# The up projections of a hybrid encoder layer: plain three-pass products in place of the seven-product scheme, and the gated first branch kept on chip

## The chip, the cores and the metric

The kernel runs on one core of a Trainium2 chip. The metric is the device time of one execution in microseconds (us). TensorE is called PE in the profile (PEld is its weight load), VectorE DVE, ScalarE ACT, GpSimd POOL and SyncE SP.

## The reference

One layer of a streaming encoder, for 528 prompt tokens (16 meta rows and 512 frames) and 64 sample tokens that share the weights; D_MODEL is 2048. All data is float32. Cut to what matters here:

```python
h = rms_norm(x, pre_gain)
(g_q, g_k, g_v, g_z, g_r, s_q, s_k, s_v, s_z, m_gla, m_sb) = jnp.split(h @ w_in, IN_SPLITS, axis=-1)
...
y_gla = (o_gla * jax.nn.silu(g_z)) @ w_up_gla
...
y_sb = (o_sb.reshape(B, T, SB_W) * jax.nn.silu(s_z)) @ w_up_sb
merged = jax.nn.sigmoid(m_gla) * y_gla + jax.nn.sigmoid(m_sb) * y_sb
y = x + rms_norm(merged @ w_o, post_gain)
```

`w_up_gla` and `w_up_sb` are 1024 x 2048 each, `w_o` is 2048 x 2048. The meta rows are dropped behind the up projections, so that these work on 576 token columns.

## The kernel before

Activations lie transposed: features on the 128 partitions, tokens in the free dimension. A float32 product is made of three passes of rounded parts: an operand is split into a high part (a cast to fp32r, "hi") and a remainder (the operand minus its high part, "lo"), and a product is hi·hi + hi·lo + lo·hi, three matmuls of 128x288 (`passes`).

The products run as *pairs* of two 128-column tiles of the output. Each pair's weights come from HBM into a `raw` tile (1 MB, three buffers) by two loads on SP. A pair is a list of *units*: a unit takes four k-tiles of weights, a 128x512 block, which ScalarE casts to `whi` and of which VectorE takes the remainder `wlo` (a ring of four each), and TensorE then multiplies. The streams `convert`, `remain`, `combine` and `multiply` issue these steps for all units of the program in order.

Pairs are computed by a Strassen-like scheme (`strassen`), with two halves of the tokens, the two column tiles and the two halves of k as the 2x2 blocks: seven products in place of eight. Its price is sums: of weight blocks (`raw<-raw` on VectorE), of products (`out`, `u` from the PSUM banks `b`), and of the activations, which are made once per operand as seven blocks (H11, H21, H22 and T1 to T4).

Stages, in order: the norm; the input projection (`w_in`), with the attention branches in the background; the up projections, first 8 pairs of `w_up_gla` (key "og"), then 8 pairs of `w_up_sb` (key "os"); and 8 pairs of `w_o`, whose results are transposed, scaled and added to x. An up pair has k = 8 tiles, so seven units of 12 matmuls. A w_o pair has 14 units.

What touches the change:

- `operands` loads the eight tiles of a branch from DRAM scratch into one `stage` tile, makes the sums (two on POOL, two on VectorE), and `split` turns each of seven blocks into hi and lo, in the places of old activation tiles (tags such as h0h; a block in the trace is `h0h`, `h6h` and so on). `RELEASE` says from which unit on such a place is free.
- `up_pair` with `done_gla` or `done_sb`: a finished column tile in `out` or `u` is multiplied by its gate (loaded from scratch as `gate`, with ScalarE's sigmoid). The first branch's result is stored to scratch (`d_yg`); in the second branch it is loaded again (`yg`), and POOL adds the two into a quarter of the merged tiles, `m_tile(0)` to `m_tile(3)` (`m<-out,yg`).
- `merged` takes those quarters as blocks of the w_o product: again sums and splits into hi and lo (`m<-m,m`); the items in `ON_POOL` are made by POOL, the others by VectorE. The order "first" of the first w_o pair begins with the blocks that are ready earliest.

What sets the order of the work is the planner (`Plan`): it keeps an estimated time for each engine and lets the stream with the earliest due time issue next (`UP_LEADS` and `WO_LEADS` shift the streams). The result is one fixed list per engine, in which an engine works strictly in order.

All instructions are recorded by one helper and have line 197 in the profile; they are told apart by their tiles.

Of the kernel before, what the change touches and what calls it, by code (L numbers as in the profile page):

```python
# [9 lines left out]
F32 = mybir.dt.float32  # L10
# [3 lines left out]
AF = mybir.ActivationFunctionType  # L14
# [3 lines left out]
P = 128  # L18
# [3 lines left out]
T = TP + DEC  # L22
# [3 lines left out]
KT = D // P  # L26
# [181 lines left out]
def hybrid_step_kernel(ctx: ExitStack, tc: tile.TileContext, a, o):  # L208
# [651 lines left out]
    opnd = {}  # L860
    halves = TO // 2

    def up_pair(src, p, key, done):
        outs, got = {}, {}
        depth = 2 if key == "og" else 3

        def put(ct, half, f, last):
            if ct not in outs:
                fourth = (2 * p + ct) % 4 == 3
                outs[ct] = pools["ev"].tile([P, T], F32, "u" if fourth else "out", bufs=1 if fourth else 3)[:, :TO]  # L870
            f(outs[ct][:, half * halves : half * halves + halves], slice(0, halves))
            if last:
                gated(ct, outs.pop(ct))

        def blocks(blk, k):
            return [x[:, k] for x in opnd[key, blk]]

        def gated(ct, t):
            done(2 * p + ct, t, got[ct], got[ct, "at"] + 0.1)

        def fetch(ct):
            got[ct] = pools[key].tile([P, TO], F32, "gate", bufs=depth)
            sync.dma_start(out=got[ct], in_=scratch["mg" if key == "og" else "ms", 2 * p + ct])
            t = got[ct, "at"] = plan.ready[got[ct].tensor.name]
            slower.append((t, "act", lambda x=got[ct]: act.activation(x, x, AF.Sigmoid), None))
            if key == "os":
                yg = pools[key].tile([P, TO], F32, "yg", bufs=depth)
                sync.dma_start(out=yg, in_=scratch["yg", 2 * p + ct])
                got[ct] = got[ct], yg

        def need(blk, q):
            first = KT if key == "os" else 0
            for b, x, c in ((H11, "stored", -4), (H21, "gated", -depth), (T1, "gated", 1 - depth), (T1, "stored", -3)):
                c += 2 * p + first
                if b == blk and c >= (first if x == "gated" else 0) and (x, c) not in made:
                    return False
            return (key, blk) in made

        strassen(src, 2 * p * P, 4, "up", blocks, halves, put, need, {"W12": lambda: fetch(0), "S1": lambda: fetch(1)})

    def done_gla(c, t, s, at):
        d = dram(("yg", c), TO)

        def f():
            dve.tensor_mul(t, t, s)
            sync.dma_start(out=d, in_=t)
            made.update(((x, c) for x in ("gated", "stored")))

        after("dve", f, slower, t=at)

    m_tiles = {}

    def m_tile(i, dtype=F32R):

        if i not in m_tiles:
            if i == 1:
                t = pools["os"].tile([P, 8 * halves], dtype, "m1")
# [5 lines left out]
    def done_sb(c, t, s, at):  # L923
        s, yg = s

        def f():
            dve.tensor_mul(t, t, s)
            after("pool", g, slower)

        def g():  # L930
            x, t2, yg2 = m_tile(c // 4, F32)[:, :, c % 4], *(z.rearrange("p (j t) -> p j t", j=2) for z in (t, yg))
            pool.tensor_add(x, t2, yg2)
            made.update((("gated", KT + c), ("stored", KT + c), ("m", c)))

        after("dve", f, slower, t=at)

    OG_TAGS = {H11: "h0h", H21: "h0l", T4: "h6h", T1: "h6l", T3: "h5h", H22: "h5l", T2: "h3h"}
    OS_TAGS = {H11: "h3l", H22: "h4h", T2: "h4l", T3: "h1h", T1: "h1l", H21: "h2h", T4: "h2l"}
    ON_POOL = (("T1", 0), ("T1", 1), (H22, 0), (T4, 0), (T3, 1))
    M_TAGS = {  # L940
        0: "h0h", 2: "h6h", 3: "h0l", (H11, 0): "h6l", (H11, 1): "h5h", (T1, 0): "h5l", (T1, 1): "h3h",
        (H21, 0): "h3l", (T4, 0): "h2l", (T3, 0): "h2h", (H22, 0): "h1l", (T2, 0): "h1h",
        (H21, 1): "h4h", (T4, 1): "h4l", (T3, 1): "h6h", (H22, 1): "h0h", (T2, 1): "h0l",
    }
    M_AFTER = {(T3, 1): ((T4, 0), (H22, 0)), (H22, 1): ((T3, 0), (T2, 0)), (T2, 1): ((T4, 1), (H22, 1))}
    RELEASE = {f"h{BLOCK_OF[x]}": n_in - 14 + 2 * i + 2 for i, x in enumerate(ORDERS["in"])}

    for p in range(8):
        up_pair(a["w_up_gla"][0], p, "og", done_gla)
    n_gla = len(units)  # L950
    for p in range(8):
        up_pair(a["w_up_sb"][0], p, "os", done_sb)
    n_up = len(units)

    RELEASE.update({OS_TAGS[BLOCK_OF[x]]: n_up - 7 + i + 1 for i, x in enumerate(ORDERS["up"])})
    wo = {}
    ends = {}

    def wo_pair(p):
# [20 lines left out]

        def free(name):
            if p == 0:
                return name == "W12" or ("m", 12 if name == "W11" else 13) in made
# [585 lines left out]
            yield from sb_chain(seq // 5, ORDER[seq % 5])  # L1569


    def split(key, blk, src, tags):
        tag = tags[blk]
# [3 lines left out]
        hi, lo = opnd[key, blk] = [t[:, x * 1152 : (x + 1) * 1152].rearrange("p (k t) -> p k t", k=4) for x in range(2)]  # L1577
        act.copy(hi, src)
        rests["dve"].append((plan.last, (key, blk), lo, src, hi))

    rests = {"dve": [], "pool": []}

    def second(eng):

        i = 0
        while True:
            yield lambda: len(rests[eng]) > i or len(done) == 4 * BLK
            if len(done) == 4 * BLK:
# [4 lines left out]
            (pool if eng == "pool" else dve).tensor_sub(lo, src, hi.bitcast(F32))  # L1593
            done.add(key)
            if key[0] != "os":
                made.add(key)

    done = set()

    def operands(key, tags):  # L1600

        x = pools["stage"].tile([P, 8, TO], F32, "stage")
        t3 = pools["stage"].tile([P, 4, halves], F32, "t3")
        for c in range(8):
            load(x[:, c], scratch[key, c])
        x11, x12, x21, x22 = (x[:, i : i + 4, j : j + halves] for i in (0, 4) for j in (0, halves))
        yield "pool"
        pool.tensor_sub(t3, x22, x12)
        yield "pool"
        pool.tensor_sub(x12, x12, x11)  # L1610
        yield from split(key, H11, x11, tags)
        yield from split(key, H21, x21, tags)
        yield (lambda: (key, H11) in done), "dve"
        dve.tensor_sub(x11, x22, x12)
        yield (lambda: (key, H21) in done), "dve"
        dve.tensor_sub(x21, x21, x11)
        for blk, src in ((T4, x21), (T1, x12), (T3, t3), (H22, x22), (T2, x11)):
            yield from split(key, blk, src, tags)
        yield lambda: (key, T2) in done

    def merged_split(blk, half, src):
        tag = M_TAGS[blk, half]
# [7 lines left out]
        rests["pool" if (blk, half) in ON_POOL else "dve"].append((plan.last, ("m", blk, half), lo, src, hi))  # L1630

    def merged():

# [42 lines left out]
    def background():  # L1676
# [29 lines left out]
        banks.quota = 1  # L1706
        plan.lead = UP_LEADS
        act.preload_act_table_set("sigmoid_and_others")
        pools["og"] = Region("og", "right")
        pools["stage"] = Region("stage", "right")  # L1710
# [4 lines left out]
        pools["stage"].close()  # L1715
        pools["os"] = Region("os", "right")
        made.update(("os", blk) for blk in range(BLK))
        for g, name in merged():
            plan.add(g, 0.0, name)

# [12 lines left out]
    def wo_open():  # L1733
        if "tl" in pools:
            return
        act.preload_act_table_set("natural_log_exp_and_others")
        for key in ("os", "og", "ev"):
# [152 lines left out]
```

## Time and profile before

| | before |
|---|---|
| runs | 1803.08, 1809.61, 1808.87 us, median 1808.87 |
| profiled execution | 1804.95 us, span 1803.1 us |
| busy share of the span | PE 92%, DVE 78%, ACT 50%, POOL 16% |
| mean granted TensorE clock | 0.968 |
| DMA | 233.57 MB, mean 130 GB/s |

The span runs from the first to the last instruction of the profiled execution; the profiled execution's own time has a little around it. Matmuls overlap one another (one is listed with some 0.3 us while the next starts 0.13 us later), so starts, and not durations, tell their rate. "idle <- X" in a row is the time that an engine waited, and what released it.

### The profile page before, as it was taken

To read this page: it belongs to the slowest core of one execution; us is meant where nothing else is said; L and a number is where in the kernel's file an instruction comes from. 1 tells how busy PE (TensorE), PEld (TensorE's weight loads), DVE (VectorE), ACT (ScalarE), POOL (GpSimd) and SP (SyncE) were. 2 spreads that over 40 slices of the span, in tenths; PEclk is the share of its full clock that TensorE was granted. 3 is DMA by queue.
4 is the path that set the end of the run, shared out by engine and by line. 5 is a ranking of instruction groups with operands and counts; after the bars stand their busy time and mean duration, and the time that the engine had idled before them with its cause. 6 is when DMAs were issued, how large, how long until landed. Compare 5 with 4: busy or idle time off the path is not lost.

```text
span 1803.1 us, 31606 instructions
## 1 busy us (share of the span) xinstructions
PE 1654.7 (92%) x11852; PEld 1592.3 (88%) x11852; DVE 1407.5 (78%) x2247; ACT 909.9 (50%) x1880; POOL 285.5 (16%) x342
## 2 busy tenths in 40 slices
PE   3799899899999999999999999999989987779995
PEld 1599899899999998999999999999989977679994
DVE  5877878786987887876666656676789999988777
ACT  4555444354444444456645554555455554445553
POOL 4600220120120120021111111111101013310002
PEclk9899899999999999999999999999999989889998
DMA  7054334334444334555454455444546654413326
GB/s 159 14 143 139 91 109 135 97 112 119 125 115 136 113 91 120 145 149 143 128 156 130 141 153 149 133 142 123 169 127 200 203 155 141 136 50 103 100 77 210
DMA packets 332068, 233.57 MB, mean 130 GB/s; under 512 B 21531, under 2 KB 297499, under 8 KB 330747
## 3 DMA queue, kind: packets, MB, share of 16 engines
q1 hardware_dynamic: 330884, 226.83, 43.8%
q10 hardware_dynamic: 1031, 4.72, 0.9%
q8 instruction: 93, 1.52, 0.4%
q14 instruction: 60, 0.49, 0.1%
HBM read 183.89 MB, written 47.62 MB: 128 GB/s over the span
## 4 chain that ended last, share of the span: by engine, by line
PE 80%; DVE 12%; issue 3%; DMA 2%; ACT 1%; POOL 1%; DVEq 0%; SPq 0%; ACTq 0%; POOLq 0%
PE b L197 80%; DVE wlo L197 4%; DVE raw L197 2%; DVE out L197 1%; DVE m L197 1%; DMA xt<-in_x_prompt 1%; DVE u L197 1%; DVE xr L197 1%; DVE x L197 0%; ACT whi L197 0%; POOL x L197 0%; DVE b L197 0%; DMA x<-d_gv 0%; DMA q<-d_gq 0%; DVE sv L197 0%
## 5 line engine op out<-in xcount | busy, mean ns | idle before, releaser
L197 ACT CAST whi<-raw 128x512 fp32r<-128x512 f32 x840 | 514.9, 620 | 593.8 <-PE b L197 430.2
L197 DVE TENSOR_TENSOR wlo<-raw,whi 128x512 fp32r<-128x512 f32 x840 | 603.2, 732 | 246.0 <-ACT whi L197 238.5
L197 DVE TENSOR_TENSOR raw<-raw 128x1024 f32<-128x1024 f32 (+2 forms) x305 | 326.9, 1074 | 8.2
L197 PE MATMUL b<-m,whi 128*128 128x288 f32 x896 | 185.1, 301 | 20.3 <-DVE m L197 8.5
L197 PEld LDWEIGHTS b<-m,whi 128*128 128x128 f32 x896 | 149.2, 195 | 21.3 <-DVE m L197 9.0
L197 PE MATMUL b<-h2h,whi 128*128 128x288 f32 (+1 forms) x416 | 128.4, 323 | 11.6 <-DVE u L197 10.7
L197 PE MATMUL b<-m,wlo 128*128 128x288 f32 x448 | 135.4, 302 | 0.8 <-DVE wlo L197 0.8
L197 PE MATMUL b<-h2l,whi 128*128 128x288 f32 (+1 forms) x416 | 122.3, 308 | 7.7 <-ACT h2l L197 6.9
L197 PE MATMUL b<-h6h,whi 128*128 128x288 f32 (+1 forms) x416 | 122.5, 308 | 6.3 <-ACT h6h L197 5.5
L197 PE MATMUL b<-h2h,wlo 128*128 128x288 f32 (+1 forms) x384 | 118.8, 309 | 6.0 <-DVE wlo L197 6.0
L197 PE MATMUL b<-h0h,whi 128*128 128x288 f32 (+1 forms) x416 | 120.9, 305 | 2.0 <-ACT whi L197 2.0
L197 PE MATMUL b<-h5h,whi 128*128 128x288 f32 (+1 forms) x416 | 122.4, 308 | 0.0
L197 PE MATMUL b<-h6l,whi 128*128 128x288 f32 (+1 forms) x416 | 118.4, 299 | 3.2 <-DVE h6l L197 3.2
L197 PE MATMUL b<-h3h,whi 128*128 128x288 f32 (+1 forms) x416 | 120.8, 304 | 0.0
L197 PE MATMUL b<-h6h,wlo 128*128 128x288 f32 (+1 forms) x384 | 115.4, 301 | 5.0 <-DVE wlo L197 5.0
L197 PE MATMUL b<-h4h,whi 128*128 128x288 f32 (+1 forms) x416 | 119.9, 302 | 0.0
L197 PE MATMUL b<-h0l,whi 128*128 128x288 f32 (+1 forms) x416 | 119.6, 302 | 0.0
L197 PE MATMUL b<-h1l,whi 128*128 128x288 f32 (+1 forms) x416 | 119.0, 300 | 0.0
L197 PE MATMUL b<-h1h,whi 128*128 128x288 f32 (+1 forms) x416 | 119.0, 300 | 0.0
L197 PE MATMUL b<-h5l,whi 128*128 128x288 f32 (+1 forms) x416 | 118.2, 298 | 0.0
L197 PE MATMUL b<-h3l,whi 128*128 128x288 f32 (+1 forms) x416 | 117.4, 296 | 0.0
L197 PE MATMUL b<-h4l,whi 128*128 128x288 f32 (+1 forms) x416 | 117.2, 296 | 0.0
(280 smaller groups left out, 4272.1 us busy)
## 6 DMA issues: line engine op xcount, KB each, us to landing
raw<-in_w_in SPq DMA_DIRECT2D x176, 512.0 KB, 5.0
raw<-in_w_o SPq DMA_DIRECT2D x32, 512.0 KB, 4.7
raw<-in_w_up_gla SPq DMA_DIRECT2D x16, 512.0 KB, 5.4
raw<-in_w_up_sb SPq DMA_DIRECT2D x16, 512.0 KB, 5.4
d_mg<-out SPq DMA_DIRECT2D x16, 288.0 KB, 2.1
d_ms<-out SPq DMA_DIRECT2D x16, 288.0 KB, 3.7
gate<-d_mg SPq DMA_DIRECT2D x16, 288.0 KB, 4.0
gate<-d_ms SPq DMA_DIRECT2D x16, 288.0 KB, 5.9
```

What stands on the lines that cost most here:

```text
L197: return real(*args, **kw)
```

## The change

Four things change in the code.

1. `plain` replaces `strassen` for the up projections: a pair is four units, each column tile's k-tiles 0 to 3 and 4 to 7. A unit multiplies its four k-tiles with both token halves, into two PSUM banks: 24 matmuls of 128x288. There are no sums of weights or products.
2. The operands are hi and lo of the tiles themselves: four blocks of two k-tiles for each branch, loaded through a `stage` tile with two buffers. No sums.
3. The gate multiplies straight from PSUM. In the first branch the product is written into the merged tiles, which now exist from the first branch on; in the second it is written over the gate, and one VectorE sum adds it to the merged tile. Store and load of `yg` are gone, and so is POOL's sum.
4. The sums and remainders of the merged blocks that POOL made are made by VectorE (`ON_POOL` is gone). The tags of the merged tiles are dealt anew.

The core of the diff:

```diff
+    GATES = 3
+    def plain(src, c0, blocks, done, need, start):
+        box = {}
+        add_load(box, "a", src, c0, 0)
+        def unit(c, q):
+            def mm(hi, lo):
+                if q == 0:
+                    start(c)
+                    for j in range(2):
+                        banks.take(box, (c, j))
+                for k in range(4):
+                    for j in range(2):
+                        xhi, xlo = blocks(4 * q + k, j)
+                        passes(box[c, j][:, :halves], hi[:, k], lo[:, k], xhi, xlo, q == k == 0, q == 1 and k == 3)
+                if q == 1:
+                    done(c, box)
...
+        units.extend(unit(c, q) for c in range(2) for q in range(2))
...
+        def start(c):
+            got[c] = pools["up"].tile([P, TO], F32, "gate", bufs=GATES)
+            sync.dma_start(out=got[c], in_=scratch["mg" if key == "og" else "ms", 2 * p + c])
...
+        def need(c, q):
+            at = 2 * p + c - GATES + (KT if key == "os" else 0)
+            return (at < 0 or ("gated", at) in made) and all((key, 2 * q + i) in made for i in range(2))
+        def done(c, box):
+            col, s = 2 * p + c, got[c]
+            m = m_tile(col // 4, F32)[:, :, col % 4]
+            def gated():
+                for j in range(2):
+                    x = s[:, j * halves : (j + 1) * halves]
+                    dve.tensor_mul(m[:, j] if key == "og" else x, box[c, j][:, :halves], x)
+                    banks.put(box, (c, j))
+                if key == "og":
+                    made.add(("gated", col))
+                else:
+                    after("dve", merge, slower)
+            def merge():
+                dve.tensor_add(m, m, s.rearrange("p (j t) -> p j t", j=2))
...
-        def f():
-            dve.tensor_mul(t, t, s)
-            after("pool", g, slower)
-        def g():
-            x, t2, yg2 = m_tile(c // 4, F32)[:, :, c % 4], *(z.rearrange("p (j t) -> p j t", j=2) for z in (t, yg))
-            pool.tensor_add(x, t2, yg2)
...
-    ON_POOL = (("T1", 0), ("T1", 1), (H22, 0), (T4, 0), (T3, 1))
...
-        x = pools["stage"].tile([P, 8, TO], F32, "stage")
-        t3 = pools["stage"].tile([P, 4, halves], F32, "t3")
-        for c in range(8):
-            load(x[:, c], scratch[key, c])
...
+        for i, tag in enumerate(tags):
+            if i > 1:
+                yield lambda: (key, i - 2) in done
+            x = pools["up"].tile([P, 2, TO], F32, "stage", bufs=2)
+            for c in range(2):
+                sync.dma_start(out=x[:, c], in_=scratch[key, 2 * i + c])
+            yield from split(key, i, x, tag)
...
-            eng = "pool" if key in ON_POOL else "dve"
-            yield (lambda: all(("m", *k) in done for k in keys)), eng
-            (pool if eng == "pool" else dve).tensor_sub(out, x, y)
+            yield (lambda: all(("m", *k) in done for k in keys)), "dve"
+            dve.tensor_sub(out, x, y)
```

Three places in the order of the instructions show it. First TensorE, in the fourth pair of the second branch; `b_...` are PSUM banks. Before, the end of one unit and the start of the next:

```order
L197 MATMUL b_16378<-h2l,whi 128x288 x2
L197 MATMUL b_16378<-h2l,wlo 128x288
L197 MATMUL b_16378<-h2l,whi 128x288 x2
L197 MATMUL b_16378<-h2l,wlo 128x288
L197 MATMUL b_16362<-h2h,whi 128x288 x2
L197 MATMUL b_16362<-h2h,wlo 128x288
L197 MATMUL b_16362<-h2h,whi 128x288 x2
L197 MATMUL b_16362<-h2h,wlo 128x288
```

Now, inside a unit:

```order
L197 MATMUL b_16187<-h4h,whi 128x288 x2
L197 MATMUL b_16187<-h4h,wlo 128x288
L197 MATMUL b_16188<-h4h,whi 128x288 x2
L197 MATMUL b_16188<-h4h,wlo 128x288
L197 MATMUL b_16187<-h4l,whi 128x288 x2
L197 MATMUL b_16187<-h4l,wlo 128x288
L197 MATMUL b_16188<-h4l,whi 128x288 x2
L197 MATMUL b_16188<-h4l,wlo 128x288
```

A bank was held for the twelve matmuls of a unit; now each three matmuls (two with the high part of the weights, one with the remainder) go to the other of two banks.

Second, VectorE in one pair of the second branch; `wlo<-raw,whi` is a weight remainder, `raw<-raw` a sum of weight blocks, `gate` the sigmoid of the gate. Before, most of a pair:

```order
L197 TENSOR_TENSOR raw<-raw 128x512 x2
L197 TENSOR_TENSOR wlo<-raw,whi 128x512
L197 TENSOR_TENSOR raw<-raw 128x512
L197 TENSOR_TENSOR out<-out,b_16790 128x288
L197 TENSOR_TENSOR u<-out,b_16750 128x288
L197 TENSOR_TENSOR out<-out,b_16733 128x288
L197 TENSOR_TENSOR u<-u 128x288
L197 TENSOR_TENSOR u<-u,b_16676 128x288
L197 TENSOR_TENSOR wlo<-raw,whi 128x512
L197 TENSOR_TENSOR raw<-raw 128x512
L197 TENSOR_TENSOR wlo<-raw,whi 128x512 x3
L197 TENSOR_TENSOR out<-out,gate 128x576
```

Now, the rows of two column tiles, as many as a pair has:

```order
L197 TENSOR_TENSOR gate<-b_16657,gate 128x288
L197 TENSOR_TENSOR gate<-b_16658,gate 128x288
L197 TENSOR_TENSOR wlo<-raw,whi 128x512
L197 TENSOR_TENSOR m_15596<-m_15596,gate 128x2x288
L197 TENSOR_TENSOR wlo<-raw,whi 128x512
L197 TENSOR_TENSOR gate<-b_16725,gate 128x288
L197 TENSOR_TENSOR gate<-b_16726,gate 128x288
L197 TENSOR_TENSOR wlo<-raw,whi 128x512
L197 TENSOR_TENSOR m_15596<-m_15596,gate 128x2x288
L197 TENSOR_TENSOR wlo<-raw,whi 128x512
```

The weight sums and the sums of products are gone; three remainders fewer are made; the gating reads the banks; and the merging sum, which POOL did, stands here.

Third, VectorE behind the last up projection, where the first w_o pair begins; `m_0_...` and `m_1_...` are hi and lo of blocks, of which the remainder is made here. Before:

```order
L197 TENSOR_TENSOR out<-out,gate 128x576
L197 TENSOR_TENSOR u<-u,gate 128x576
L197 TENSOR_TENSOR m_16427<-m_16427 128x1152
L197 TENSOR_TENSOR wlo<-raw,whi 128x512 x2
L197 TENSOR_TENSOR m_16729<-m_17334,m_16729 128x1152
L197 TENSOR_TENSOR m_16729<-m_16729 128x1152
L197 TENSOR_TENSOR wlo<-raw,whi 128x512 x2
L197 TENSOR_TENSOR raw<-raw 128x512 x2
L197 TENSOR_TENSOR wlo<-raw,whi 128x512
L197 TENSOR_TENSOR raw<-raw 128x512 x2
L197 TENSOR_TENSOR m_0_17444<-m_16427,m_0_17444 128x1152
```

Now:

```order
L197 TENSOR_TENSOR gate<-b_17065,gate 128x288
L197 TENSOR_TENSOR gate<-b_17066,gate 128x288
L197 TENSOR_TENSOR m_15855<-m_15855,gate 128x2x288
L197 TENSOR_TENSOR m_15334<-m_15855,m_15334 128x1152
L197 TENSOR_TENSOR m_15334<-m_15334 128x1152
L197 TENSOR_TENSOR wlo<-raw,whi 128x512 x3
L197 TENSOR_TENSOR raw<-raw 128x512 x3
L197 TENSOR_TENSOR wlo<-raw,whi 128x512 x3
L197 TENSOR_TENSOR m_0_17142<-m_15056,m_0_17142 128x1152
L197 TENSOR_TENSOR m_0_17163<-m_15056,m_0_17163 128x1152
L197 TENSOR_TENSOR m_1_17166<-m_15855,m_1_17166 128x1152
```

The two gatings (behind five sums of products, and with POOL's sums still to come) have become two products and a merging sum, all on VectorE; the remainders of `m` (POOL's among them) now stand closer together in VectorE's list, behind six weight remainders.

More of the change, by code (lines that the diff above doesn't have):

```diff
@@ L861, in hybrid_step_kernel @@
     halves = TO // 2
[L863 to L899, printed above, removed]
@@ L901, in done_gla @@
-    def done_gla(c, t, s, at):
-        d = dram(("yg", c), TO)
-        def f():
-            dve.tensor_mul(t, t, s)
-            sync.dma_start(out=d, in_=t)
-            made.update(((x, c) for x in ("gated", "stored")))
-        after("dve", f, slower, t=at)
+    GATES = 3
[14 more added lines that the diff above has]
+                    done(c, box)
+            return {
+                "src": lambda: box["a"][:, c, 4 * q : 4 * q + 4],
+                "mm": mm,
+                "post": next_load if c == q == 1 else None,
+                "need": lambda: need(c, q),
+                "from": lambda: 0.0,
+                "prep": 0,
+                "loaded": lambda: "a" in box,
+                "banks": 2 if q == 0 else 0,
+            }
+        units.extend(unit(c, q) for c in range(2) for q in range(2))
@@ new lines, in up_pair, with blocks @@
+    def up_pair(src, p, key):
+        got = {}
+        def blocks(k, j):
+            return [x[:, k % 2, j * halves : (j + 1) * halves] for x in opnd[key, k // 2]]
+        def start(c):
+            got[c] = pools["up"].tile([P, TO], F32, "gate", bufs=GATES)
+            sync.dma_start(out=got[c], in_=scratch["mg" if key == "og" else "ms", 2 * p + c])
+            got[c, "at"] = plan.ready[got[c].tensor.name]
+            slower.append((got[c, "at"], "act", lambda x=got[c]: act.activation(x, x, AF.Sigmoid), None))
+        def need(c, q):
[15 more added lines that the diff above has]
+                dve.tensor_add(m, m, s.rearrange("p (j t) -> p j t", j=2))
+                made.update((("gated", KT + col), ("m", col)))
+            after("dve", gated, t=got[c, "at"] + 0.7)
+        plain(src, 2 * p * P, blocks, done, need, start)
@@ L916, in m_tile @@
             if i == 1:
-                t = pools["os"].tile([P, 8 * halves], dtype, "m1")
+                t = pools["up"].tile([P, 8 * halves], dtype, "m1")
             else:
@@ L982, in free @@
             if p == 0:
[L983 removed]
+                return True
             if name == "W11" and "tl" not in pools:
@@ L1576, in split @@
         t = block(tag)
-        hi, lo = opnd[key, blk] = [t[:, x * 1152 : (x + 1) * 1152].rearrange("p (k t) -> p k t", k=4) for x in range(2)]
+        hi, lo = opnd[key, i] = [t[:, x * 1152 : (x + 1) * 1152].rearrange("p (k t) -> p k t", k=2) for x in range(2)]
         act.copy(hi, src)
-        rests["dve"].append((plan.last, (key, blk), lo, src, hi))
-    rests = {"dve": [], "pool": []}
+        rests["dve"].append((plan.last, (key, i), lo, src, hi))
+    rests = {"dve": []}
     def second(eng):
@@ L1586, in second @@
         while True:
-            yield lambda: len(rests[eng]) > i or len(done) == 4 * BLK
-            if len(done) == 4 * BLK:
+            yield lambda: len(rests[eng]) > i or len(done) == 2 * BLK + 8
+            if len(done) == 2 * BLK + 8:
                 return
@@ L1592, in second @@
             yield eng
-            (pool if eng == "pool" else dve).tensor_sub(lo, src, hi.bitcast(F32))
+            dve.tensor_sub(lo, src, hi.bitcast(F32))
             done.add(key)
-            if key[0] != "os":
-                made.add(key)
+            made.add(key)
     done = set()
     def operands(key, tags):
-        x = pools["stage"].tile([P, 8, TO], F32, "stage")
-        t3 = pools["stage"].tile([P, 4, halves], F32, "t3")
-        for c in range(8):
-            load(x[:, c], scratch[key, c])
[L1606 to L1619, printed above, removed]
+        for i, tag in enumerate(tags):
+            if i > 1:
+                yield lambda: (key, i - 2) in done
+            x = pools["up"].tile([P, 2, TO], F32, "stage", bufs=2)
+            t = plan.last
+            for c in range(2):
+                sync.dma_start(out=x[:, c], in_=scratch[key, 2 * i + c])
+            plan.last = max(t, plan.ready[x.tensor.name])
+            yield from split(key, i, x, tag)
+        yield lambda: (key, len(tags) - 1) in done
     def merged_split(blk, half, src):
@@ L1629, in merged_split @@
         act.copy(hi, src)
-        rests["pool" if (blk, half) in ON_POOL else "dve"].append((plan.last, ("m", blk, half), lo, src, hi))
+        rests["dve"].append((plan.last, ("m", blk, half), lo, src, hi))
     def merged():
@@ L1708, in background @@
         act.preload_act_table_set("sigmoid_and_others")
-        pools["og"] = Region("og", "right")
-        pools["stage"] = Region("stage", "right")
+        pools["up"] = Region("up", "right")
         for eng in rests:
@@ L1714, in background @@
         yield from operands("os", OS_TAGS)
-        pools["stage"].close()
-        pools["os"] = Region("os", "right")
-        made.update(("os", blk) for blk in range(BLK))
         for g, name in merged():
@@ L1736, in wo_open @@
         act.preload_act_table_set("natural_log_exp_and_others")
-        for key in ("os", "og", "ev"):
+        for key in ("up", "ev"):
             pools[key].close()
```

27 lines of the change are left out of this document (10 added, 17 removed).

## The prediction

> **What bounds the kernel now.** I read the stages first (busy time in stretches), then who TensorE waited for, then the costs on VectorE, then single rows. The change touches only the stretch from 1341 us, where the up projections begin, to 1616 us, where the first pair of the w_o product ends.
>
> Busy time in stretches; after the start and length come busy us of PE, PEld, DVE, ACT and POOL with the number of instructions, then the granted TensorE clock, the DMA share and GB/s:
> ```profile
> core 0: us, PE busy (x) PEld busy (x) DVE busy (x) ACT busy (x) POOL busy (x), PEclk, DMA share, GB/s
> 1341.00:1443.00 102.00, 93.99 (x676) 92.65 (x676) 96.72 (x148) 57.05 (x102) 6.11 (x2) 0.95 0.62 193
> 1443.00:1566.00 123.00, 100.00 (x673) 95.63 (x672) 116.90 (x153) 61.89 (x107) 35.59 (x16) 0.92 0.49 150
> 1566.00:1616.60 50.60, 29.45 (x171) 28.19 (x170) 44.57 (x44) 20.21 (x28) 13.44 (x5) 0.76 0.21 58
> 1616.60:1781.20 164.60, 164.19 (x1254) 163.72 (x1252) 130.83 (x272) 87.80 (x267) 1.69 (x1) 1.00 0.38 107
> ```
> The rows are the GLA half of the up projections, the stick-breaking half, the first w_o pair and the other w_o pairs. In the last, TensorE never stops and has its full clock: it is the bound there. In the second and third it idles and runs at a lower clock, while VectorE is busy 95% of the second.
>
> TensorE's own timeline gives the price of work. The first up matmul, the second unit (12 matmuls) of one pair, the first unit of the next pair, the first w_o matmul, and the first of the second w_o pair:
> ```profile
> 1341.09 0.43 PE L197 MATMUL b<-h0h,whi 128*128 128x288 f32 x2
> ...
> 1361.17 0.42 PE L197 MATMUL b<-h6h,whi 128*128 128x288 f32 x2
> ...
> 1370.69 0.42 PE L197 MATMUL b<-h0h,whi 128*128 128x288 f32 x2
> ...
> 1565.89 0.43 PE L197 MATMUL b<-m,whi 128*128 128x288 f32 x2
> ...
> 1616.45 0.43 PE L197 MATMUL b<-m,whi 128*128 128x288 f32 x2
> ```
> From 1361.17 to 1370.69 stand six units, 72 matmuls without a wait: 9.52 us, so 0.1322 us for one and 1.587 us for a unit. The up projections are 16 pairs of 7 units, 1344 matmuls, 177.7 us of work, and take 1565.89 - 1341.09 = 224.8 us: 47.1 us are lost. The first w_o pair is 14 units, 22.2 us, and takes 50.6: 28.4 lost. What TensorE waited for between 1341 and 1617 us (total, times, longest):
> ```profile
> PE b L197 <- DVE wlo L197: 18.3, 15, 2.5
> PE b L197 <- DVE m L197: 8.5, 2, 4.3
> PE b L197 <- ACT h2l L197: 6.9, 1, 6.9
> PE b L197 <- POOL m L197: 6.3, 1, 6.3
> PE b L197 <- ACT m L197: 5.5, 1, 5.5
> PE b L197 <- ACT h6h L197: 4.2, 1, 4.2
> ```
> Together 49.7 us; the rest of the list is under 1 us each. The rows on m belong to the w_o pair (20.3 of its 28.4), the others, 29.4, to the up stage (of its 47.1). The remainder, some 8 and 18 us, is slow clock behind the waits. After one of them three matmuls take 0.72 us instead of 0.40:
> ```profile
> 1349.07 0.68 PE L197 MATMUL b<-h6h,whi 128*128 128x288 f32 x2
> 1349.55 0.44 PE L197 MATMUL b<-h6h,wlo 128*128 128x288 f32 x1
> 1349.79 0.68 PE L197 MATMUL b<-h6h,whi 128*128 128x288 f32 x2
> ```
> That is 0.24 us a matmul; over the w_o pair's four long waits and a short one the 8 us come to about 1.7 for each.
>
> **The change part by part.** Groups of instructions from 1341 to 1566 us (count, busy us and mean ns of one, then idle time before them):
> ```profile
> L197 DVE TENSOR_TENSOR wlo<-raw,whi 128x512 fp32r<-128x512 f32 x111 | 80.1, 745 | 4.2 <-ACT whi L197 4.2
> L197 ACT CAST whi<-raw 128x512 fp32r<-128x512 f32 x112 | 69.1, 621 | 76.9 <-DVE raw L197 38.0 <-PE b L197 35.2 <-ACT out L197 1.3
> L197 DVE TENSOR_TENSOR raw<-raw 128x512 f32<-128x512 f32 x63 | 57.4, 912 | 2.2
> L197 ACT ACTIVATE gate<-gate 128x576 f32<-128x576 f32 x31 | 20.9, 682 | 1.0 <-DMA gate<-d_mg 0.5 <-DMA gate<-d_ms 0.5
> L197 DVE TENSOR_TENSOR out<-out,b 128x288 f32<-128x288 f32 x46 | 20.8, 452 | 1.9 <-PE b L197 0.5
> L197 DVE TENSOR_TENSOR out<-out,gate 128x576 f32<-128x576 f32 x23 | 19.4, 857 | 0.0
> L197 DVE TENSOR_TENSOR m<-m,m 128x1152 fp32r<-128x1152 f32 x5 | 6.7, 1346 | 0.0
> L197 ACT CAST m<-m 128x1152 fp32r<-128x1152 f32 x5 | 5.8, 1156 | 0.0
> ```
> *TensorE.* A pair becomes 4 units of 24 matmuls (4 k-tiles, 2 halves, 3 passes): 96 instead of 84, 1536 in all. At 0.1322 that is 203.1 us, +25.4. All of it lies on the path.
>
> *VectorE in the up stage.* Before, a pair costs 7 wlo, 4 weight sums, 5 sums of products and 2 gatings: by the means 5.2 + 3.6 + 2.3 + 1.7 = 12.8 us, against 11.1 of TensorE. VectorE is the bound. Now a pair costs 4 wlo and 4 products with the gate out of PSUM. That product of a 128x288 bank has no row; between the sum with a bank (0.452) and twice that, I take 0.452, since it has the same operands. So 3.0 + 1.8 = 4.8 us in the GLA half. The other half adds two merging sums of 128x576 (nearest row: the gating, 0.857): 6.5 us. Every second pair also gives one sum and two remainders of 128x1152 (1.346 each), 2 us a pair: 8.5 us under 12.7 of TensorE. Twice the product's price makes 10.3, still covered. What hides VectorE's work now is TensorE; the cover is 4 us a pair.
>
> *ScalarE.* 7 casts, 3 copies and 2 sigmoids become 4 casts and 2 sigmoids, 3.8 us a pair: hidden. A sigmoid waits for its gate's load and holds the casts behind it; the ring of four whi is now four units of 3.17 us ahead, 12.7 us, which covers a load of 6.5 us at most (below).
>
> *Transfers.* Gone are 16 stores and 16 loads of 288 KB of the gated first branch (issued on SP, where the weight loads queue too). Nothing of that was on TensorE's list; I cost it at nothing. Gate loads stay, one a column of 6.3 us. With three buffers the third before must be consumed first, so a load is issued two columns ahead.
>
> *The start.* The operand tiles now come one after the other through two stage buffers, the fourth behind a weight load and behind the remainder of the second. That weight load on SP:
> ```profile
> 1337.68 0.99 SPq L197 DMA_DIRECT2D raw<-in_w_up_gla  x2
> ```
> The time from issue to landing (min/median/max) of the stage loads, and of the gate loads:
> ```profile
> DMA to landing us min/median/max: 5.2/5.9/6.0
> ```
> ```profile
> DMA to landing us min/median/max: 2.6/4.6/6.5
> ```
> On this clock the fourth tile is issued at 1338.8 and there at 1344.8; a cast and a remainder of 128x1152 (1.16 and 1.35) end at 1347.3. TensorE, started at 1341.1, wants it one and a half of its new units later (4.76 us), at 1345.9. Wait 1.5, slow clock up to 1.7: I take 3 us; from 0 (it lands sooner) to 7 (as the old wait on h6h, 5.0, with its slow clock). The wait at the second operand set (h2l, 6.9) goes: its loads are issued in the first half's time, 100 us ahead.
>
> *Before the start.* POOL's two sums on stage go. The second of them, and what TensorE waited for from 1283 to 1341 us:
> ```profile
> 1297.72 2.98 POOL L197 TENSOR_TENSOR stage<-stage 128x1152 f32<-128x1152 f32 x1
> ```
> ```profile
> PE b L197 <- DVE wlo L197: 1.9, 2, 1.2
> ```
> Both waits lie beside these sums. So -2 us; between 0 and, with gaps too short for the list, -2.5.
>
> *From the last up matmul to w_o.* VectorE's queue behind it holds 2 products (0.9), the merge (0.8), 2 sums (2.7), 6 wlo and 3 weight sums (0.69 each, row below: 6.2), then the remainder m5 (1.35): done 12 us after the last matmul. TensorE has five units ready, 7.9 us, and then waits 4, and 1.7 of slow clock. Two remainders, a sum, two wlo, two weight sums, a remainder, one wlo and a remainder later comes m6_1, after 22.6; TensorE wants it at about 21.6, so 1 more, and at the last unit half a microsecond, with a little slow clock: 8 us lost, the pair takes 30. Bounds: 0, and the 28.4 of now. Now the same work is dearer because POOL shares it: a VectorE row beside a POOL row, and then a wlo later, with POOL idle:
> ```profile
> 1580.49 3.81 DVE L197 TENSOR_TENSOR m<-m,m 128x1152 f32<-128x1152 f32 x1
> ...
> 1606.63 0.69 DVE L197 TENSOR_TENSOR wlo<-raw,whi 128x512 fp32r<-128x512 f32 x1 [0.99 <-ACT whi L197]
> ```
> ```profile
> 1576.96 6.13 POOL L197 TENSOR_TENSOR m<-m,m 128x1152 fp32r<-128x1152 f32 x2
> ```
> 3.81 instead of 1.35. POOL has nothing left to do in this stage, so I price VectorE's rows undisturbed. Five items move from POOL to VectorE, 6.7 us, which are in the list above.
>
> **Sum.** 203.1 + 3 + 30.2 = 236.3 us against 275.4 (1341.09 to 1616.45): -39. With the 2 us ahead: -41. The profiled execution took 1804.95 us, so 1764. The median shown is 1808.87, 3.9 above it, the fastest run 1803.08; half-way between profiled run and median gives +2: 1766.
>
> **The rivals.**
> *A, the gap before w_o stays* (28.4 lost, not 8): 1786. For it: the remainders now all stand in VectorE's queue, behind three weight sums that nobody needs yet. Against it: the longest wait there ends on POOL, and POOL's sums slow VectorE's rows there.
> *B, no gap at all*: both waits hidden, 1766 - 11 = 1755.
> *C, the up stage is not VectorE's.* If its 47 us came from loads and queues, they stay, and 25.4 come on top: 1804.95 - 2 + 25.4, less the 20 of the gap, 1808; 1828 if the gap stays too. The change loses from the point at which over 52 us stay lost in both places (225.3 of matmuls and these make 277.4, the old time and the 2 us ahead). Against it: no load stands on TensorE's list, and the waits on wlo follow VectorE at 95%.
> *D, the clock does not hold.* Each three matmuls change the bank now, where the old units hold one for twelve. If that let the clock fall, a matmul would cost up to 0.24: half of them slow makes 0.186, +82 us, 1848; the gain is gone at 0.159 on average. The last stretch above ran 1254 matmuls at 1.00 with a bank held for twelve, so no row shows it either way. The Trainium skill ("TensorE: Matmul & The Clock Gate", "A second HAM failure mode: psum-queue depth-cycling") reports a kernel that cycled PSUM banks at each iteration, idled briefly in between and had its clock go up and down; by that rule rival D happens. Here the next bank is taken long before it is needed, so I see no idle time for it to come from.
>
> **How the numbers follow.** Forecast 0.62, A 0.13, B 0.16, C 0.05, D 0.04. Own spread of the forecast: start 0 to 7, gap 4 to 14, product price nil, the median +-3: 1757 to 1776. The range takes in A and B: 1750 to 1788, and leaves out C, D and some tails. About 0.5%, 9 us, is what a measurement of this kernel tells from no change. Slower comes from D and a part of C: 0.06; the same from the rest of C: 0.03; faster 0.91.
>
> **What would show it.** Right: TensorE busy near 100% at clock 1.00 over some 203 us of up projections, VectorE near 60%, no wait on wlo there; POOL idle; waits left at the fourth operand tile and at m5 in the sixth w_o unit, 2 and 4 us. Wrong: a clock below 1 inside the up stage without idle time (D), waits on gate or raw loads (C), or over 15 us of waits on m (A).

## The result and the profile after

| | before | after |
|---|---|---|
| median of four runs | 1805.97 us (the three runs above and one of 1801.58) | 1762.36 us (1758.87 to 1764.55) |
| ratio | | 0.976, 95% interval 0.973 to 0.979 |
| profiled execution's span | 1803.1 us | 1757.1 us |
| first up matmul | 1341.09 | 1335.22 |
| first w_o matmul | 1565.89 | 1540.48 |
| second w_o pair | 1616.45 | 1570.38 |

The change took 43.6 us off the median. The spans differ by 46.0: 5.9 lie ahead of the up stage, 19.5 in it (224.8 to 205.3), 20.7 in the first w_o pair (50.6 to 29.9), and from the second w_o pair to the end it is the same (186.7 in both).

Busy time in stretches, after: the two halves of the up stage, the first w_o pair, and the next 164.6 us (columns as in the prediction):
```profile
core 0: us, PE busy (x) PEld busy (x) DVE busy (x) ACT busy (x) POOL busy (x), PEclk, DMA share, GB/s
1335.22:1438.94 103.72, 102.09 (x771) 101.65 (x770) 43.06 (x71) 34.93 (x53) 0.00 (x0) 1.00 0.56 166
1438.94:1540.48 101.54, 101.54 (x770) 101.54 (x769) 61.80 (x93) 36.57 (x55) 0.00 (x0) 1.00 0.44 127
1540.48:1570.38 29.90, 24.83 (x170) 23.90 (x169) 27.90 (x35) 16.70 (x24) 0.00 (x0) 0.94 0.25 69
1570.38:1735.00 164.62, 164.29 (x1255) 163.87 (x1253) 130.85 (x271) 87.89 (x267) 1.61 (x1) 1.00 0.37 107
```
In the second row TensorE has no idle time at all: 768 matmuls of 0.1322 us are 101.5. VectorE, 95% busy here before, is busy 61%, and POOL has nothing to do in any of the first three rows. In the third, VectorE is busy 27.9 of 29.9 us; whether it bounds that pair still is tested in experiment 9.

All that TensorE waited for from 1330 to 1600 us (total, times, longest), where before it was 49.7 us in six rows:
```profile
PE b L197 <- DVE m L197: 2.9, 1, 2.9
PE b L197 <- ACT out L197: 1.4, 1, 1.4
PE b L197 <- DVE h6l L197: 1.0, 1, 1.0
PE b L197 <- DVE wlo L197: 0.7, 1, 0.7
PE b L197 <- ACT h6l L197: 0.6, 1, 0.6
```
VectorE's groups from the first up matmul to the first w_o matmul; these four are now most of its work:
```profile
L197 DVE TENSOR_TENSOR wlo<-raw,whi 128x512 fp32r<-128x512 f32 x65 | 45.0, 692 | 54.4 <-ACT whi L197 50.8 <-DMA stage<-d_os 2.5
L197 DVE TENSOR_TENSOR m<-b,gate 128x288 f32<-128x288 f32 x32 | 13.2, 452 | 24.7 <-PE b L197 24.7
L197 DVE TENSOR_TENSOR gate<-b,gate 128x288 f32<-128x288 f32 x30 | 12.3, 452 | 17.5 <-PE b L197 16.9 <-ACT gate L197 0.4
L197 DVE TENSOR_TENSOR m<-m,gate 128x576 f32<-128x576 f32 x15 | 11.3, 752 | 0.0
```
The idle time before these rows ends on TensorE's banks, or on the casts that wait for its ring: VectorE follows TensorE now.

### The profile page after: what moved, and what is told of

It reads as the page before. It is cut to its first block, busy times and chain, and to the rows that moved or that the text cites. A ratio compares the mean times of both kernels' runs of the same rounds, so it can differ in the third digit from the quotient of the medians.

```text
span 1757.1 us, 31515 instructions
## 1 busy us (share of the span) xinstructions
PE 1656.8 (94%) x12044; PEld 1599.5 (91%) x12044; DVE 1274.7 (73%) x2098; ACT 859.8 (49%) x1778; POOL 225.5 (13%) x317
## 4 chain that ended last, share of the span: by engine, by line
PE 86%; DVE 8%; DMA 2%; issue 1%; ACT 1%; POOL 1%; SPq 0%; DVEq 0%; ACTq 0%; POOLq 0%
PE b L197 86%; DVE wlo L197 2%; DVE raw L197 1%; DMA xt<-in_x_prompt 1%; DVE x L197 1%; DVE xr L197 1%; DMA d_og<-x 0%; ACT whi L197 0%; POOL x L197 0%; DVE b L197 0%; DVE u L197 0%; SPq L197 0%; DMA stage<-d_og 0%; DVE m L197 0%; DMA q<-d_gq 0%
## 5 line engine op out<-in xcount | busy, mean ns | idle before, releaser
L197 ACT CAST whi<-raw 128x512 fp32r<-128x512 f32 x792 | 485.5, 620 | 628.7 <-PE b L197 504.8
L197 DVE TENSOR_TENSOR wlo<-raw,whi 128x512 fp32r<-128x512 f32 x792 | 558.0, 716 | 294.7 <-ACT whi L197 282.8
L197 DVE TENSOR_TENSOR raw<-raw 128x1024 f32<-128x1024 f32 (+2 forms) x241 | 266.6, 1109 | 6.0
L197 PE MATMUL b<-h4h,whi 128*128 128x288 f32 (+1 forms) x480 | 132.8, 301 | 0.0
L197 PE MATMUL b<-h1h,whi 128*128 128x288 f32 (+1 forms) x480 | 131.9, 299 | 0.0
L197 PE MATMUL b<-h4l,whi 128*128 128x288 f32 (+1 forms) x480 | 130.1, 296 | 0.0
L197 PE MATMUL b<-h1h,wlo 128*128 128x288 f32 (+1 forms) x416 | 123.5, 297 | 1.5 <-DVE wlo L197 1.5
L197 PE MATMUL b<-h4h,wlo 128*128 128x288 f32 (+1 forms) x416 | 123.4, 297 | 1.6 <-DVE wlo L197 1.6
L197 PE MATMUL b<-h0h,wlo 128*128 128x288 f32 (+1 forms) x416 | 123.4, 297 | 0.7 <-DVE wlo L197 0.7
L197 PE MATMUL b<-h2h,whi 128*128 128x288 f32 (+1 forms) x352 | 111.7, 317 | 10.7 <-DVE u L197 10.7
```

Source lines behind the costliest of these rows:

```text
L197: return real(*args, **kw)
```

## Experiments

"The stretch" below is the time from the end of the last up matmul to the second w_o pair; in every kernel but one (experiment 6) the first w_o matmul follows the last up matmul at once. Its matmuls are 22.2 us. Experiments 4, 5 and 7 and the first kernel of 8 have one execution each, so there the readings rest on the trace more than on the total.

**1. What bound the up stage: no weight sums.**
```diff
-        for sums in ((("W11", "S3", s3), ...), (("W22", "S2", s2), ...)):
+        for sums in ((("W11", "S3", s3), ...), (("W22", "S2", s2), ...))[: 0 if kh == 4 else 2]:
```


> The kernel before, with the 64 weight sums of the 16 up pairs left out (its up projections are then not the reference's; everything else stands as it was, the 1344 matmuls, the round trip of the gated first branch, the five items on POOL). Theory 1, VectorE bounds the up stage: its work falls from 12.8 to 9.2 us a pair, under the 11.1 of TensorE, so the waits on wlo (18.3 us) and their slow clock go; what stays are 177.7 us of matmuls and the waits for the operand sets (4.2 and 6.9, with slow clock 14): some 192 us for the up stage instead of 224.8. Theory 2 (rival C), loads and queues bound it: about 225 again. For the first w_o pair: if its 28.4 us of loss come from POOL's rows and what they do to VectorE, it stays at 45 to 51 us; if they are arrears that VectorE carries over from the up stage, it falls to 30 to 38.

1765.55 us, ratio 0.978 (0.977 to 0.980). The up stage fell from 224.8 to 189.6 us, so 35 of its 47 us of loss came of VectorE's weight sums (with POOL emptied too, in experiment 6, it is 182.0, 4 us above its matmuls); rival C is out. I had let the waits for the operand sets stand (14 us with slow clock); 0.9 of them is left, so these too came of VectorE's queue. Its second half and the stretch:
```profile
1433.28:1529.88 96.60, 91.58 (x675) 89.26 (x673) 91.72 (x117) 55.85 (x101) 31.63 (x16) 1.00 0.58 181
1529.88:1576.19 46.31, 29.88 (x170) 28.18 (x169) 42.62 (x44) 19.98 (x28) 12.93 (x5) 0.78 0.28 76
```
The stretch hardly fell, to 46.3, which by the expectation spoke for POOL. Leaving 64 sums out brings nearly what the change brings; but the changed kernel's up stage is 15.7 us longer than this one, for its 25.4 us of added matmuls, and its stretch is 16.4 us shorter. So the stretch became the question.

**2. The five items back on POOL, in the changed kernel.**
```diff
+    ON_POOL = (("T1", 0), ("T1", 1), (H22, 0), (T4, 0), (T3, 1))
-        rests["dve"].append(...)
+        rests["pool" if (blk, half) in ON_POOL else "dve"].append(...)
```
(and so for the sums.)

> The changed kernel with the five merged-block items (two sums' and three remainders' places) back on POOL, as the kernel before had them; nothing else differs. Theory 1, the gap before w_o closed because POOL stands empty: the first w_o pair goes from 29.8 back towards 40 to 50 us, with a wait on POOL in TensorE's list, 10 us or more on the total. Theory 2, the gap closed because VectorE no longer carries arrears out of the up stage: the pair stays within 30 to 34 us, 0 to 4 us on the total.

1764.05 us, ratio 0.977 (0.976 to 0.979); stretch 31.2 us. Theory 2. POOL does hold up VectorE, as a remainder on POOL and then two wlo beside it show:
```profile
1560.98 3.88 POOL L197 TENSOR_TENSOR m<-m,m 128x1152 fp32r<-128x1152 f32 x1 [14.99 <-ACT m L197]
```
```profile
1562.23 3.78 DVE L197 TENSOR_TENSOR wlo<-raw,whi 128x512 fp32r<-128x512 f32 x2
```
The two wlo take 3.78 us where two alone took 1.29. The Trainium skill ("SBUF — State Buffer", "Who interferes with whom") says that a VectorE instruction with two SBUF inputs contends with a POOL instruction that reads SBUF, and these rows agree. Yet TensorE felt only 1.3 us of it.

**3. The round trip restored.**
```diff
+                yg[c] = pools["ev"].tile([P, T], F32, "out", bufs=3)[:, :TO]
+                sync.dma_start(out=yg[c], in_=scratch["yg", 2 * p + c])
...
+                    sync.dma_start(out=dram(("yg", col), TO), in_=s)
...
-                dve.tensor_add(m, m, s...)
+                dve.tensor_add(m, yg[c]..., s...)
```


> The changed kernel, but the gated first branch is stored to memory and loaded again beside its second branch's gate, as in the kernel before (16 stores and 16 loads of 288 KB more, issued on the queue of the weight loads; three buffers that stand idle in this stage take the loads). Theory 1, the round trip is hidden: up stage 205 us again, total within 3 us of the changed kernel (0.976 of before). Theory 2, the transfers or their place in the queue count: waits on raw or gate loads appear and the up stage grows by 5 us or more.

1761.0 us, ratio 0.976 (0.974 to 0.978); up stage 205.3, stretch 29.9. Theory 1: keeping the first branch on chip moved nothing that TensorE waits for.

**4. Gating from a copy instead of from PSUM.**
```diff
+                    act.copy(y[:, j * halves : (j + 1) * halves], box[c, j][:, :halves])
...
-                    dve.tensor_mul(m[:, j] if key == "og" else x, box[c, j][:, :halves], x)
+                dve.tensor_mul(m if key == "og" else x, y..., x)
```


> The changed kernel, but the products leave their banks by a copy on ScalarE (two of 128x288 a column, 0.40 us each) and are gated from that copy by one VectorE product of 128x576. Theory 1, gating straight from the bank saves nothing that TensorE waits for: up stage 205 to 206, the first w_o pair up to 1 us longer, total within 3 us of the changed kernel. Theory 2, it is part of the gain: 5 us or more.

1763.1 us, stretch 29.95, second half 101.55. The up stage took 207.0, 1 us beyond what I gave; what it has over the changed kernel lies in the first half, at the start wait and in the slow clock behind it (below). Theory 1.

**5. A bank held for twelve matmuls.** In `plain`, `for j` outside `for k`.

> The changed kernel with the two loops of a unit exchanged: each bank is held for 12 matmuls, instead of changing after every three. Theory 1: the bank's change costs nothing, 6.347 us a column of 48 matmuls as now, up stage within 1 us of 205. Theory 2 (what is left of rival D): a change of bank costs a little; 10 ns at each would be 5 us less in the up stage.

1762.13 us. The second half took 101.97 us against 101.54: the bank's change costs nothing. The up stage as a whole took 208.2, outside what either theory gave; 2.6 of the 3 us are again in the first half, behind the start wait.

**6. POOL emptied in the kernel before, without and with the weight sums.** `ON_POOL = ()`, and the merging sum `pool.tensor_add(x, t2, yg2)` by `dve`.

> The kernel before without the weight sums of the up pairs (as in the run without them: up stage 189.6 us, first w_o pair 46.3), and now with the merging sums and the five merged-block items on VectorE, so that POOL has nothing to do at the end of the up stage. Theory 1, POOL's rows make the gap before w_o, by being slow themselves and by holding up VectorE's rows: the pair falls to 32 to 37 us (the changed kernel's 29.9, and 3.7 more of sums and gatings behind the last up matmul), total 9 to 14 us less than without the weight sums alone. Theory 2, the gap comes from the pair's form, which ends both its columns with its last unit: the pair stays at 42 to 46.

> The kernel before, weight sums kept, with the merging sums and the five merged-block items on VectorE instead of POOL. Theory 1, the gap is POOL's: the first w_o pair falls from 50.6 to 33 to 40 us, while the up stage, bound by VectorE, takes on up to 12 us of merging sums: total -12 to +6. Theory 2, the gap is arrears of a VectorE that is the bound: with 19 us more on it the pair stays at 48 or more and the total grows by 10 us or more.

Without weight sums: 1759.69 us, ratio 0.976 (0.974 to 0.977); up stage 182.0. Its second half runs at TensorE's own pace (89.1 us for 672 matmuls), and the stretch is 46.9:
```profile
1523.97:1570.85 46.88, 24.37 (x170) 23.81 (x169) 40.45 (x48) 20.04 (x27) 0.00 (x0) 0.75 0.21 56
```
POOL is at 0.00, and the stretch has not shrunk: theory 1 is out, and 46.9 lies just above what theory 2, the pair's form, gave. With the weight sums: 1790.66 us, ratio 0.994 (0.992 to 0.995). Up stage and stretch of that kernel:
```profile
1439.64:1547.90 108.26, 93.62 (x674) 91.23 (x672) 101.06 (x163) 58.22 (x103) 0.00 (x0) 0.95 0.57 174
1547.90:1600.42 52.52, 26.64 (x169) 25.29 (x169) 47.91 (x54) 24.36 (x31) 0.00 (x0) 0.71 0.18 48
```
Here the first w_o matmul itself waits 11.1 us for a merged block, so the stretch begins at 1547.9: 52.5 us, longer than before's 50.6. The pair is as theory 2 had it, the total (13 us less) as neither. The up stage fell to 209.9. VectorE's rows run undisturbed there (in the second half a weight sum has a mean of 0.69 us against 0.99 before, a remainder 0.69 against 0.81), and merging work was put off to the end. So POOL cost the kernel before some 12 us in all, but emptying it does not close the gap. VectorE's rows in the stretch show why, first before, then with POOL emptied:
```profile
L197 DVE TENSOR_TENSOR wlo<-raw,whi 128x512 fp32r<-128x512 f32 x15 | 13.6, 928 | 3.9 <-ACT whi L197 3.9
L197 DVE TENSOR_TENSOR raw<-raw 128x512 f32<-128x512 f32 x10 | 9.2, 924 | 0.2
L197 DVE TENSOR_TENSOR m<-m,m 128x1152 fp32r<-128x1152 f32 x6 | 8.0, 1353 | 0.4 <-ACT m L197 0.4
L197 DVE TENSOR_TENSOR m<-m,m 128x1152 f32<-128x1152 f32 x4 | 7.9, 1968 | 0.1
L197 DVE TENSOR_TENSOR m<-m 128x1152 f32<-128x1152 f32 x2 | 3.9, 1958 | 0.0
```
```profile
L197 DVE TENSOR_TENSOR m<-m,m 128x1152 fp32r<-128x1152 f32 x14 | 18.5, 1353 | 0.0
L197 DVE TENSOR_TENSOR wlo<-raw,whi 128x512 fp32r<-128x512 f32 x15 | 10.1, 687 | 3.0 <-ACT whi L197 3.0
L197 DVE TENSOR_TENSOR raw<-raw 128x512 f32<-128x512 f32 x8 | 5.4, 690 | 0.6 <-DMA raw<-in_w_o 0.4
L197 DVE TENSOR_TENSOR m<-m,m 128x1152 f32<-128x1152 f32 x4 | 5.4, 1357 | 0.1
L197 DVE TENSOR_TENSOR m<-m 128x1152 f32<-128x1152 f32 x4 | 5.4, 1353 | 0.0
```
With POOL idle the rows are shorter, some 9.6 us by the means over before's counts, but VectorE has ten rows on merged blocks more to do there, 13.5 us; three of them POOL had done.

**7. Items and merging sums on POOL, in the changed kernel**: experiment 2, and `after("pool", merge, slower)` with `pool.tensor_add`.

> The changed kernel with the five merged-block items and the merging sums of the second branch on POOL, as the kernel before had both. With the items alone the first w_o pair took 31.2 us. Theory 1, the merging sums on POOL make the gap: the pair takes 36 to 46 us. Theory 2, the form of the last pair makes it: 31 to 34. The up stage stays at 205 to 208 either way.

1764.42 us; stretch 31.3. As theory 2 gave it, and the same as with the items alone: the merging sums on POOL do not make the gap either.

**8. More work on VectorE, in the changed kernel.**
```diff
+                x = pools["up"].tile([P, TO], F32, "x")
+                for i in range(2):   # 5 in the second kernel
+                    dve.tensor_add(x, s, s)
```


> The changed kernel with two sums of 128x576 more on VectorE behind the products of each column (0.75 us each, into a tile that nobody reads): 24 us more in each half, 67 and 86 us of some 102. Theory 1, TensorE is the bound and VectorE's cover holds: up stage 205 to 207; the first w_o pair 1.5 us longer, since the last column's two stand in front of the merge. Theory 2, the cover is nearly used up already, by bursts or by the ring of four units: 10 us or more in the up stage.

> As with two sums more for each column, but five: 60 us more on VectorE in each half, 103 us of some 103 in the first and 122 us of some 102 in the second. Theory 1, the stage's time is the larger of TensorE's and VectorE's work: 0 to 4 us more in the first half, 20 more in the second and up to 35 with the slow clock that comes with waits, 4 to 8 in the first w_o pair: 27 to 45 us on the total. Theory 2, VectorE's work does not set the time of such a stage: under 6 us.

With two: 1767.94 us. The second half stays at 101.55 us with VectorE at 80.9 of it, so the cover holds; but the stretch grows to 35.5, by 5.6 instead of 1.5, since three rows on merged blocks more (4.1 us) are left for it. VectorE had 20.7 us free in that half, so lack of time alone does not explain them; the fixed order may have a part, which no run here separates. With five: 1809.59 us, ratio to before 1.004 (1.003 to 1.005), so the gain is gone (some 47 us more than the changed kernel, forecast 27 to 45):
```profile
1443.83:1571.16 127.33, 110.58 (x771) 109.66 (x770) 108.38 (x162) 34.53 (x53) 0.00 (x0) 0.92 0.35 102
1571.16:1618.35 47.19, 24.30 (x170) 23.75 (x169) 42.73 (x51) 19.20 (x26) 0.00 (x0) 0.75 0.16 42
```
The first half took 110.6 (+6.9, forecast 0 to 4), the second 127.3 (+25.8, forecast 20 to 35), and the stretch 47.2, as long as in the kernel before: here I had forecast 4 to 8 us and got 17.3. Of VectorE's 14.8 us more in the stretch, 6.8 are nine of the added sums, five of them of the last column, and 6.8 five rows on merged blocks. The form of the pair is the changed kernel's, and POOL is idle; the gap is back because VectorE is late. So it needs neither POOL nor the old form of the pair. All kernels, by the stretch (us), VectorE's busy time in it, and the number of its rows on merged blocks (128x1152) that are still to be done there:

| kernel | stretch | VectorE busy | rows on merged blocks |
|---|---|---|---|
| before, POOL emptied | 52.5 | 47.9 | 22 |
| before | 50.6 | 44.7 | 12, and 3 on POOL |
| after, five sums more | 47.2 | 42.7 | 15 |
| before, no weight sums, POOL emptied | 46.9 | 40.5 | 16 |
| before, no weight sums | 46.3 | 42.6 | 10, and 3 on POOL |
| after, two sums more | 35.5 | 33.4 | 13 |
| after, items and merging on POOL | 31.3 | 30.1 | 9, and 2 on POOL |
| after, items on POOL | 31.2 | 29.7 | 9, and 2 on POOL |
| after, gating from a copy | 30.0 | 26.5 | 11 |
| after | 29.9 | 27.9 | 10 |
| after, round trip | 29.9 | 27.9 | 10 |
| after, banks held | 28.5 | 27.7 | 10 |
| after, other order (9) | 27.3 | 26.9 | 10 |
| after, no w_o sums (9) | 26.5 | 23.5 | 10 |

In every one the stretch is VectorE's busy time and 0.4 to 6.4 us more: it follows the work that VectorE still has to do when the up stage ends. The old form of the pair counts here too: with POOL emptied it gives VectorE some 3.6 us of sums, gatings and merging more behind its last matmul (an estimate from the means of its rows).

**9. Can the rest be had?** A kernel with other leads (`combine` at -0.3 in `UP_LEADS`; `convert` 0.2, m1 and m2 0, m3 -0.3 and back 0.3 in `WO_LEADS`), and one with the first w_o pair's eight weight sums left out (`[: 0 if kind == "first" else 2]`).

> The changed kernel with other leads for the planner at the end of the up stage: the sums and remainders of the merged blocks are spread between the casts and remainders of w_o's weights, and the remainder m5 stands ahead of weight sums that are needed later. Theory 1, what is left of the gap (29.9 us for 22.2 of matmuls) is the order on VectorE and ScalarE: the pair takes 26 to 28 us, total 2 to 4 us under the changed kernel. Theory 2, the work behind the last up matmul is too long for any order, a wait only changes its place: 29 to 31.

> The changed kernel with the eight weight sums of the first w_o pair left out (that pair's product is then not the reference's): 5.5 us less on VectorE beside that pair, which keeps it busy 27.9 us of the pair's 29.9, against 22.2 of matmuls. Theory 1, VectorE is the bound of the first w_o pair in the changed kernel too: the pair falls to 23 to 26 us, and the total by 4 to 7 us under the changed kernel. Theory 2, what is left is a chain (last product, merge, two sums, cast, remainder) that no lighter VectorE shortens: 28 to 30.

Other order: 1759.26 us, ratio 0.976 (0.975 to 0.978); stretch 27.3, up stage 203.1. The stretch:
```profile
1542.14:1569.48 27.34, 23.68 (x170) 22.41 (x169) 26.94 (x34) 16.78 (x24) 0.00 (x0) 1.00 0.21 60
```
VectorE fills it, and the clock holds. The trace shows the 2.6 us in the stretch, but the ratio is no lower than the change's own 0.976, so as a faster kernel it is not shown. The up stage has no start wait (203.1 is its matmuls alone), but two waits of 1.0 and 0.2 us stand ahead of it instead, and behind the second w_o pair's start 187.3 us follow, not 186.7: a part of what the order gains in one place it loses in others. Without the eight sums: 1756.7 us, ratio 0.974 (0.971 to 0.977), stretch 26.5, half a microsecond above theory 1's range and below theory 2's. VectorE sheds 4.4 us and the stretch 3.4, so VectorE bounds that pair still for the most part; one wait of 2.5 for a remainder stays, so a chain is a part of it.

## Why the prediction held, point by point

- *The matmuls.* +25.4 us: right to a few tenths.
- *VectorE in the up stage.* The product from PSUM took 0.452, the value taken; the merge 0.752 (taken 0.857). A pair cost VectorE 5.4 us in the first half and 7.7 in the second (4.8 and 8.5 forecast). No wait for wlo or for a gate was left in the stage.
- *The start.* The fourth operand tile was waited for as forecast, 0.64 for its cast and 0.99 for its remainder; 2.2 us were lost with what lies around (3 forecast), since no slow clock followed.
- *Before the start.* Mis-sized: 5.9 us instead of 2. Of these 3.1 are not the change's. The last store on SP ahead of the first instruction in which the two programs differ stands at 1281.01 in before and 1277.88 in after. That place moves between kernels whose edits come only later (1275.86 to 1282.56 in the ten changed kernels), so that it fell on the good side is luck. From that store to the first up matmul it is 60.1 us before and 57.3 after, and 57.3 in nine of the ten changed kernels; the 2.7 us between fit the waits on wlo beside POOL's sums (1.9 us), which are gone, and their slow clock.
- *The gap.* 7.7 us lost, 8 forecast, but with other parts. Rows of TensorE in the first w_o pair:
```profile
1546.35 0.40 PE L197 MATMUL b<-m,wlo 128*128 128x288 f32 x1 [0.69 <-DVE wlo L197]
1552.57 0.40 PE L197 MATMUL b<-m,whi 128*128 128x288 f32 x1 [2.90 <-DVE m L197]
1560.45 0.53 PE L197 MATMUL b<-m,whi 128*128 128x288 f32 x2 [1.45 <-ACT out L197]
```
  VectorE's rows behind the last up matmul; m5 is the first of the four that start at 1551.16:
```profile
1541.31 0.81 DVE L197 TENSOR_TENSOR gate<-b,gate 128x288 f32<-128x288 f32 x2
1542.15 0.76 DVE L197 TENSOR_TENSOR m<-m,gate 128x576 f32<-128x576 f32 x1
1542.95 1.36 DVE L197 TENSOR_TENSOR m<-m,m 128x1152 f32<-128x1152 f32 x1
1544.34 1.36 DVE L197 TENSOR_TENSOR m<-m 128x1152 f32<-128x1152 f32 x1
1545.62 1.89 DVE L197 TENSOR_TENSOR wlo<-raw,whi 128x512 fp32r<-128x512 f32 x3
1547.42 2.02 DVE L197 TENSOR_TENSOR raw<-raw 128x512 f32<-128x512 f32 x3
1549.35 1.89 DVE L197 TENSOR_TENSOR wlo<-raw,whi 128x512 fp32r<-128x512 f32 x3
1551.16 5.28 DVE L197 TENSOR_TENSOR m<-m,m 128x1152 fp32r<-128x1152 f32 x4
```
  And ScalarE's two casts and the copy behind them:
```profile
1557.90 2.20 ACT L197 CAST m<-m 128x1152 fp32r<-128x1152 f32 x2
1560.01 0.39 ACT L197 COPY out<-b 128x288 f32<-128x288 f32 x1
```
  m5 ended 11.9 us behind the last up matmul (12 forecast). The wait for it was 2.90 (4 forecast), with slow clock behind it as forecast. The waits at m6_1 and at the last unit did not come; in their place stand two that I had not looked for: the fourth unit's wlo, behind the two sums of merged blocks, and a bank's copy on ScalarE, queued behind two casts of merged blocks. I had read VectorE's list only, and not ScalarE's. So the path and the first long wait were right, and that the sum came within 0.3 us is in part luck.
- *Why the gap was there before.* This reason was wrong, though its size came out. I wrote that the work "is dearer because POOL shares it". Dearer it was, by some 9.6 us of VectorE's time, but emptying POOL left the gap (experiment 6), and filling it again cost 1.3 and 1.4 us (2 and 7). The gap was work on merged blocks that VectorE had still to do when the up stage ended; the forecast of 30.2 held because it was summed from VectorE's remaining rows.
- *Rivals.* A: the gap did close. B: it did not vanish. C: out by experiment 1, and from the other side by 8. D: the clock stayed at 1.00 in both halves with the bank changed at every third matmul, and holding it did no better (5). The cycling of banks of which the Trainium skill tells ("TensorE: Matmul & The Clock Gate", "A second HAM failure mode: psum-queue depth-cycling") goes with short idle times; there were none here, so no run shows the two together.

For the profiled execution the forecast was 1764, and 1758.87 came. Of these 5.1 us, 3.1 are the earlier part's, and start, gap and what lies ahead of the start make 0.8, 0.3 and 0.7. The median lies 3.5 above the profiled execution, for which I had counted 2.

## What to carry to other kernels

A scheme that saves one matmul in eight is no gain where its sums fall on the engine that is already the bound: compare the two engines' work per pair, not their sums over the span. Work on an engine that is hidden while the stage runs is not free for that: it can push other work behind the stage's end, in front of the next one. How much it pushes depends on the engine's free time and on the order of its list. To size such a gap, list what stands in every engine's queue behind the last matmul, the casting engine's as well as the subtracting one's.

## What the runs showed of the hardware

The slow clock behind a wait is not fixed by the wait. The same wait, 2.7 us on `cs` in a part that both programs share, stands in both traces; the busy time in stretches around it, before and then after:
```profile
400.00:410.00 10.00, 7.49 (x43) 7.12 (x44) 6.10 (x15) 3.41 (x8) 0.80 (x1) 0.83 0.09 34
```
```profile
400.00:410.00 10.00, 8.89 (x64) 8.21 (x64) 6.08 (x14) 3.61 (x8) 0.81 (x1) 1.00 0.10 38
```
The granted clock is 0.83 in the one and 1.00 in the other. And the wait of 2.90 us in the first w_o pair stands in the changed kernel and in the one with banks held: in the first, a run of 14 matmuls at 0.24 us followed it, in the second no such run did, and that stretch is 1.4 us shorter. At the start of the up stage likewise: where the two waits for the fourth tile came to 1.3 to 1.7 us (six kernels) no slow matmuls followed; at 1.8 to 2.2 (three kernels: gating from a copy, banks held, two sums more) they did, and the first half took 105.4 to 106.3 us, where five of the six took 103.4 to 103.8 (the sixth is the one with five sums more). The tenth, with the other order, has no such wait and took 101.6. The Trainium skill ("TensorE: Matmul & The Clock Gate", "What's actually happening") says that activity is judged in a window that runs free of the program; that agrees with a wait that is punished in one run and not in another. So 1.7 us behind a wait, as the prediction counted, is a likely price and not a sure one.
